# Two layers of a hybrid decoder: the weight sums' steps planned with a longer latency, and h's copy to DRAM written earlier in the FFN

## The chip, the core and the metric

The kernel runs on one core of a Trainium2 chip. A core has five engines that run side by side, each through its own queue of instructions in order: PE (TensorE, matmuls), DVE (VectorE), ACT (ScalarE), POOL (GpSimd) and SP (SyncE, which here only issues DMAs). They wait for each other by semaphores. POOL also issues DMAs; those that add to what stands in DRAM all come from it. The metric is the device time of one execution in microseconds (us), lower is better, as the median of several runs.

## The reference

The reference is two layers of a decoder on 16 + 512 = 528 positions of width 1024, all in float32. Each layer has a mixer and an FFN:

```python
u = rms_norm(h, pre_g); z = u @ w_in                    # mixer
q, k, v, f_logit, a_val, a_gate, sc_b, sc_c, sc_x = split(z)
y = concat[forgetting_attention(q, k, v, log_sigmoid(f_logit + b)),   # 8 heads of 64
           silu(layer_norm(conv31(a_val * sigmoid(a_gate)))) @ a_pw_w,
           sc_b * conv3(sc_c * sc_x)]
h = h + rms_norm(head_rms_norm(y) @ w_out, post_g)

z = conv3(rms_norm(h, ffn_pre_g) @ w_up)                # FFN, 2 x 2816 columns
g, up = split(z)
h = h + rms_norm((silu(g) * up) @ w_down, ffn_post_g)
```

The attention's logits are q.k/8 plus a running sum of log f, with a causal mask and a softmax. The output is h without the 16 first positions.

## The kernel before

**Matmuls.** Every float32 weight and every activation is split in two parts, hi and lo, and a product is three matmuls (hi*hi, hi*lo, lo*hi; `mm3`, L837). A weight block of 512 KB comes from DRAM by a DMA of SP into a tile raw, ACT casts it to whi, DVE subtracts to get wlo.

**Mixer.** `mixer` plans its work with `Flow`, a planner in Python that runs before the kernel: each operation has an engine, a planned duration, a priority, what it comes after, and `lat`, which is added to its planned end before what depends on it may be planned. The planner so fixes the order of the instructions on PE, DVE, ACT and POOL (`tc.manual_schedule`). The attention of a head has two passes. In `maxima` PE multiplies k by q (L1593), DVE takes the maximum of each row (mcol, L1600), POOL writes it on a diagonal (dm, L1608), and PE turns that into a row by a matmul with ones (L1617), which ACT puts into q as one more row (L1619). In `exponentials` PE multiplies again (L1637), ACT takes the exponential (pf, or p for the last 16 positions, L1644), POOL clears what lies above the causal diagonal (L1651), and PE multiplies by v (L1671). Between them PE runs the projections of q, k, v and the gates (L837, L1407). SP copies rows of q and k between partitions (L1499).

**FFN.** The 2816 columns are 22 pairs of blocks f (gate and up), in parts of 8, 7 and 7; behind each part come the down products of that part. 9 pairs in the first layer and 12 in the second (`SEVEN`) are computed by `seven_pair` with seven half products in place of eight (Strassen's scheme), which needs sums of weight blocks and of activations. The sums of activations are made by `normalised`, a generator of steps that `build` takes in small lots, five behind each of the first f, and the rest in the first down product; a step `None` ends a lot. From the end of part 0 on, h's tile serves as room for weight blocks, so h is copied to DRAM (h_dram, two DMAs of SP, L2385) and read back later (L2357).

**Weight sums.** A sum for pair f is a DRAM tile w_sum{layer}_{f}: SP copies three blocks into it (L545), then three accumulating DMAs of POOL follow (L534), each of which waits until the one before has landed. In the mixers these four steps are operations of the planner: 3 sums in the first mixer (11, 12, 13) and 4 in the second (10 to 13). In the plan, sum i is not begun before `SUM_EVERY * i` us, a step of POOL takes `SUM_US`, and the next one comes at least `SUM_LAT` behind it (L1846 to L1850). POOL's queue runs in order, so what stands behind an accumulate that waits for a landing waits too. The other sums are made in the FFNs (`tick`, `down_sums`) and are not planned by `Flow`.

Of the kernel before, what the change touches and what calls it, by code (L numbers as in the profile page):

```python
# [18 lines left out]
KD = D // P  # L19
# [13 lines left out]
        ((8, 9), (10, 11, 12, 13), (15, 16), (17, 18), (19, 20)))  # L33
SEVEN = tuple(sorted(sum(places, ())) for places in SUMS)
NEXT_SUMS, AHEAD_SPLITS = 13, (8, 8, 9, 9, 10, 10, 11)
SUM_US, SUM_LAT, SUM_EVERY = 0.9, 9.0, 40.0
K2 = KD // 2
SB = K2 * P
AHEAD = 2
# [350 lines left out]
def tile_hybrid_trunk(ctx: ExitStack, tc: tile.TileContext, xT, wflat, pv_d, out):  # L390
    nc = tc.nc
# [3 lines left out]
    def T(pool, shape, dt, tag, bufs=None):  # L395
        uid[0] += 1
        kw = {} if bufs is None else {"bufs": bufs}
        return pool.tile(list(shape), dt, tag=tag, name=f"{tag}_{uid[0]}", **kw)
# [83 lines left out]
    flow = Flow()  # L482
# [17 lines left out]
    h_dram = T(dram, [P, KD, L], F32, "h_dram")  # L500
# [25 lines left out]
    def sum_steps(l, f):  # L526

        gate, up = (flat_w(up_chunk[l, t]) for t in (f, NF + f))
        t = T(dram, [P, 4, SB], F32, f"w_sum{l}_{f}")
        n, o = P * 2 * SB, offs[up_chunk[l, f]]  # L530
        diag = wflat[o:o + 2 * (n + SB)].rearrange("(e q) -> e q", e=2)[:, :n].rearrange("e (p s) -> p e s", p=P)[:, :, :SB]

        def put(to, src):
            nc.gpsimd.dma_start(to, src, accum_op=ALU.add)  # L534

        def last():
            put(t[:, 3], t[:, 2])
            sums[l, f] = t

        moves = [(t[:, 0], up[:, :SB]), (t[:, 1], up[:, :SB]), (t[:, 2:4], gate.rearrange("p (e s) -> p e s", e=2))]  # L540

        def copies():
            with tc.issue_after(last_load[0].ins):
                for to, src in moves:
                    nc.sync.dma_start(to, src)  # L545

        return copies, lambda: put(t[:, 0:2], diag), lambda: put(t[:, 2], t[:, 1]), last

    def sums_at(l, place):

        return SUMS[l][place] if l < DEPTH else ()
# [143 lines left out]
    def gp(us, fn, *after, **kw):  # L695
        return flow.op("pool", us, fn, after, **kw)
# [428 lines left out]
    def mixer(l, ypool, first, close_first, spans, front, rzs, u_at):  # L1125
# [719 lines left out]

        for i, f in enumerate(sums_at(l, 1)):  # L1846
            copies, *adds = sum_steps(l, f)
            tok = flow.op("sp", 2.0, copies, (Tok(flow.pe + SUM_EVERY * i),), prio=8, lat=SUM_LAT)
            for op in adds:
                tok = gp(SUM_US, op, tok, prio=8, lat=SUM_LAT)  # L1850

# [177 lines left out]
    with tc.tile_pool(name="pre", bufs=2, reuse_waits="tile") as sp, tc.manual_schedule(engines=every):  # L2029
# [7 lines left out]
        h, h_at = load_h(sp, xT)  # L2037
# [56 lines left out]
    for l in range(DEPTH):  # L2094
# [23 lines left out]
        with tc.tile_pool(name=f"fp{l}", bufs=2, reuse_waits="tile") as fp:  # L2118
# [35 lines left out]
            with tc.manual_schedule(engines=every):  # L2154
                flow.yields = YF
                h, h_at = load_h(fp, xT if l == 0 else h_dram)
# [40 lines left out]
            seven = SEVEN[l]  # L2197
# [12 lines left out]
            def normalised():  # L2210

                pools.pop().close()
                st = ExitStack()
                pools.append(st)
                tp = tx[0] = st.enter_context(tc.tile_pool(name=f"tp{l}", bufs=1, side="right", reuse_waits="tile"))
                tiles = [T(tp, [P, 2, K2, n7], F32R, f"t{i}") for i in range(4)]
                gpre = gains("ffn_pre_g")
                skip = 2 * n7 - (L - i0)
                b11, b12, b21, b22 = blocks = [(k0, h7[hf]) for k0 in (0, K2) for hf in range(2)]

                def un(b, k):
                    k0, (a, z) = b
                    a += skip * (b in (b12, b22))
                    nc.vector.scalar_tensor_tensor(yp[:, k0 + k, a:z], in0=h[:, k0 + k, a:z], scalar=gpre[:, k0 + k:k0 + k + 1],
                                                   in1=rz[:, a:z], op0=ALU.mult, op1=ALU.mult)

                def at(b):
                    k0, (a, z) = b
                    return yp[:, k0:k0 + K2, a:z]

                def block(k):
                    c = (slice(None), slice(k, k + 2), slice(i0, L))
                    nc.scalar.copy(uhi[c], yp[c])
                    nc.vector.tensor_sub(ulo[c], yp[c], uhi[c].bitcast(F32))

                raw = {}

                def total(i, k, x, y, op=ALU.subtract):
                    raw[i] = T(fp, [P, 2, H], F32, "acc", 2)[:, :, :n7]
                    a, b = (t if t.shape[1] == 2 else t[:, k:k + 2] for t in (x(), y()))  # L2240
                    nc.vector.tensor_tensor(raw[i], in0=a, in1=b, op=op)

                def split(i, k):
                    hi, lo = (tiles[i][:, b, k:k + 2] for b in range(2))
                    nc.scalar.copy(hi, raw[i])
                    nc.vector.tensor_sub(lo, raw[i], hi.bitcast(F32))

                for b in (b12, b22, b11, b21):
                    for k in range(K2):
                        yield lambda b=b, k=k: un(b, k)  # L2250
                for k in range(0, K2, 2):
                    if k:
                        yield None
                        yield lambda: block(0)
                        yield None
                    yield lambda: total(2, k, lambda: at(b12), lambda: at(b22))
                    yield lambda: split(2, k)
                    yield lambda: total(0, k, lambda: at(b11), lambda: at(b12))
                    yield lambda: total(1, k, lambda: at(b22), lambda: raw[0], ALU.add)
                    yield lambda: split(0, k)  # L2260
                    yield lambda: total(3, k, lambda: at(b21), lambda: raw[1])
                    yield lambda: split(1, k)
                    yield lambda: split(3, k)
                for k in range(2, KD, 2):
                    yield lambda k=k: block(k)
                    yield None
                ts.extend((t[:, 0], t[:, 1]) for t in tiles)

            mul_ins, glo_ins, ghi_ins = [None], [None], {}
            ts, n_seven, primed = [], [0], set()  # L2270
            building = [None]

            def build(n):

# [64 lines left out]
            def finish_pair():  # L2339
                if late_ups:  # L2340
                    late_ups.popleft()()
# [3 lines left out]
            for part, nf in enumerate(PARTS):  # L2345
                for f in range(f0, f0 + nf):
                    if g:
                        tick(g[max(g)][0][:, :1])
                    for _ in range(AHEAD_SPLITS.count(f) if l == 0 else 0):
                        store_one()  # L2350
                    if f in seven:
                        seven_pair(f)
                        if f == seven[-1]:
                            spare[0] = None
                            with tc.issue_after(last_load[0].ins):
                                for k in range(0, KD, 2):
                                    nc.sync.dma_start(h[:, k:k + 2], h_dram[:, k:k + 2])  # L2357
                        continue
                    finish_pair()
                    if seven and f == 2:  # L2360
                        building[0] = normalised()
                    for i in (2 * f, 2 * f + 1):
                        if i < len(zs):
                            continue
                        if i < FIRST["w_out"]:
                            scaled(i, [first.ps[hf, i] for hf in range(2)])
                            continue
                        w = next_w()
                        ps = mmt((6, 2)[i % 2]) if ts else mmt()
                        mm3({hf: ps[:, hf, :iws[hf]] for hf in range(2)}, w, range(KD), u_in)  # L2370
                        if ts:
                            for (a, z), hf in zip(i_spans, range(2)):
                                nc.scalar.copy(zs[i % len(zs)][:, off + a - i0:off + z - i0], ps[:, hf, :z - a])
                            continue
                        scaled(i, [ps[:, :, :H]] if i0 == 0 else [ps[:, hf, :iws[hf]] for hf in range(2)])
                    g[f] = ffn_gate(f)
                    if building[0] is not None and f < PARTS[0] - 1:
                        with tc.issue_after(mul_ins[0].ins):
                            build(5)
                finish_pair()  # L2380
                ks = list(range(nf))
                grhs = lambda b, k, hf, f0=f0: g[f0 + k][b][:, fw * hf:fw * (hf + 1)]
                if seven and part == 0:
                    for k in range(0, KD, 4):
                        nc.sync.dma_start(h_dram[:, k:k + 4], h[:, k:k + 4])  # L2385
                    spare[0] = h
                if part < len(PARTS) - 1:
                    more = down_sums(l, part)
# [102 lines left out]
```

## Time and profile before

| | us |
|---|---|
| median of 3 runs | 1263.06 |
| lowest, highest | 1262.32, 1263.31 |
| profiled execution | 1262.1 |
| its span | 1260.4 |
| first mixer, about | 55 to 215 |
| first FFN with w_out and down products, about | 215 to 684 |
| second mixer, about | 684 to 842 |
| second FFN, about | 842 to 1260 |

The span runs from the first instruction to the last. In the prediction a row of a timeline is: start, duration, engine, line, operation, output <- inputs, sizes, and in brackets how long the engine was idle before it and what ended the wait. A row of waits is: engine, what it waited to start, for whom, then the total, how often, and the longest. A row of stretches is: the stretch, its length, then busy time and count for PE, PEld (weight loads), DVE, ACT and POOL, the granted clock of PE, the share of the DMA engines, and GB/s. A row of one line's instructions gives the least, median and longest duration in ns.

### The profile page before, as it was taken

What the parts mean: (1) busy time and instruction counts of PE and PEld (TensorE: products, weight loads), DVE (VectorE), ACT (ScalarE), POOL (GpSimd) and SP (SyncE); (2) the same over time, 40 slices, a digit from 0 to 9 for tenths busy, and PEclk for the clock granted to TensorE, in tenths of its full rate; (3) what the DMA queues carried; (4) which work ended last, traced back from release to release, by engine and by line L of the source; (5) the groups of instructions that cost most, each with busy time, mean ns of one, the idle gap of its engine ahead of it and who ended that gap; (6) DMA issues with size and microseconds to landing.
All of it is one profiled execution on the core that took longest, in us unless ns stands there. A gap on an engine that the chain in (4) does not pass through costs nothing.

```text
span 1260.4 us, 24292 instructions
## 1 busy us (share of the span) xinstructions
PE 1244.2 (99%) x9554; PEld 1194.4 (95%) x9554; DVE 926.0 (73%) x1581; ACT 710.3 (56%) x1377; POOL 175.9 (14%) x360
## 2 busy tenths in 40 slices
PE   8999999999999999999999999999999999999997
PEld 8999898999999999999999988999999899989997
DVE  7887866589874776487688877756799748757954
ACT  7254576655444663476673545775554447526763
POOL 1323411001111001010003244110022000000000
PEclk9999999999999999999999999999999999999999
DMA  7267551726658755765652684547166565465611
GB/s 245 80 154 180 122 118 47 256 88 150 185 146 339 243 192 153 243 193 169 209 186 68 157 194 109 144 116 238 70 166 177 148 212 172 151 228 178 203 60 67
DMA packets 80755, 206.59 MB, mean 164 GB/s; under 512 B 8624, under 2 KB 18992, under 8 KB 80128
## 3 DMA queue, kind: packets, MB, share of 16 engines
q1 hardware_dynamic: 66976, 168.20, 42.1%
q0 software_dynamic: 13664, 36.84, 13.0%
q8 instruction: 75, 1.23, 0.4%
q14 instruction: 40, 0.33, 0.1%
HBM read 170.82 MB, written 50.60 MB: 176 GB/s over the span
## 4 chain that ended last, share of the span: by engine, by line
PE 94%; DVE 2%; ACT 1%; DMA 1%; POOL 1%; issue 0%; SPq 0%; DVEq 0%; ACTq 0%
PE psum L837 63%; PE psum L2288 17%; PE psum L1407 5%; PE psum L1671 3%; PE psum L1637 2%; PE psum L974 1%; PE psum L1593 1%; PE psum L1737 1%; PE psum L1323 1%; DMA raw<-in_w_dram 0%; POOL dm L1608 0%; DMA h<-in_x_dram 0%; DVE yp L1050 0%; DVE h L1060 0%; PE psum L1617 0%
## 5 line engine op out<-in xcount | busy, mean ns | idle before, releaser
L837 PE MATMUL psum<-y,whi 128*128 128x264 f32 (+3 forms) x1968 | 383.8, 299 | 0.8 <-DVE zs L989 0.7
L837 PEld LDWEIGHTS psum<-y,whi 128*128 128x128 f32 x1968 | 305.8, 188 | 13.7 <-DVE zs L989 0.9
L837 PE MATMUL psum<-uhi,whi 128*128 128x264 f32 (+1 forms) x1168 | 292.2, 289 | 1.5 <-ACT uhi L2069 0.8
L837 PE MATMUL psum<-ulo,whi 128*128 128x264 f32 (+1 forms) x1168 | 286.0, 284 | 0.6 <-DVE ulo L2071 0.4
L837 PE MATMUL psum<-uhi,wlo 128*128 128x264 f32 (+1 forms) x1168 | 285.3, 284 | 0.0
L837 PE MATMUL psum<-y,wlo 128*128 128x264 f32 (+3 forms) x984 | 274.0, 297 | 0.7 <-DVE wlo L793 0.7
L837 PEld LDWEIGHTS psum<-uhi,whi 128*128 128x128 f32 x1168 | 201.7, 189 | 5.9 <-issue 1.6
L837 PEld LDWEIGHTS psum<-ulo,whi 128*128 128x128 f32 x1168 | 201.8, 189 | 1.3 <-DVE ulo L2071 0.6
L837 PEld LDWEIGHTS psum<-uhi,wlo 128*128 128x128 f32 x1168 | 201.5, 189 | 0.0
L837 PEld LDWEIGHTS psum<-y,wlo 128*128 128x128 f32 x984 | 178.0, 188 | 6.4 <-DVE wlo L793 1.1
L2173 DVE SCALAR_TENSOR_TENSOR c<-zs,pv,c 128x528 f32<-128x528 f32 (+1 forms) x176 | 130.5, 756 | 21.2 <-ACT c L2171 19.9
L652 ACT CAST whi<-raw 128x1024 fp32r<-128x1024 f32 (+1 forms) x65 | 66.1, 1021 | 96.9 <-PE psum L837 74.3
L793 DVE TENSOR_TENSOR wlo<-raw,whi 128x1024 fp32r<-128x1024 f32 (+2 forms) x80 | 95.6, 1204 | 31.1 <-ACT whi L789 30.5
L789 ACT CAST whi<-raw 128x1024 fp32r<-128x1024 f32 (+2 forms) x80 | 81.7, 1030 | 26.3 <-PE psum L837 18.1
L653 DVE TENSOR_TENSOR wlo<-raw,whi 128x1024 fp32r<-128x1024 f32 (+1 forms) x65 | 76.9, 1183 | 20.9 <-ACT whi L652 20.9
L1153 DVE SCALAR_TENSOR_TENSOR cacc<-apad,pv,cacc 128x528 f32<-128x528 f32 x120 | 87.5, 771 | 0.1
L2288 PE MATMUL psum<-uhi,whi 128*128 128x258 f32 (+1 forms) x252 | 71.4, 284 | 0.0
L2288 PE MATMUL psum<-ulo,whi 128*128 128x258 f32 (+1 forms) x252 | 71.3, 283 | 0.0
L2288 PE MATMUL psum<-uhi,wlo 128*128 128x258 f32 (+1 forms) x252 | 70.8, 283 | 0.0
L2171 ACT ACTIVATE c<-zs,pv 128x528 f32<-128x528 f32 (+1 forms) x88 | 63.0, 727 | 6.8 <-DVE zs L2136 2.6
L2206 POOL COPY cols<-y 128x1 f32<-128x1 f32 x24 | 18.4, 767 | 334.7 <-ACT y L2187 334.4
L2288 PE MATMUL psum<-t,shi 128*128 128x258 f32 (+1 forms) x336 | 63.2, 283 | 0.0
(273 smaller groups left out, 2324.4 us busy)
## 6 DMA issues: line engine op xcount, KB each, us to landing
raw<-in_w_dram SPq DMA_DIRECT2D x114, 512.0 KB, 4.6
raw<-in_w_dram SPq DMA_DIRECT2D x30, 448.0 KB, 5.2
h<-in_w_dram SPq DMA_DIRECT2D x25, 512.0 KB, 4.7
raw<-w_sum SPq DMA_DIRECT2D x21, 512.0 KB, 5.2
h<-w_sum SPq DMA_DIRECT2D x21, 512.0 KB, 5.1
h<-in_w_dram POOLq DMA_DIRECT2D x16, 512.0 KB, 4.0
w_sum<-h POOLq DMA_DIRECT2D x16, 512.0 KB, 6.3
w_sum<-in_w_dram SPq DMA_DIRECT2D x26, 256.0 KB, 5.8
```

The lines of the kernel that those rows point to most:

```text
L652: nc.scalar.copy(hi[:, :sz], raw[:, :sz])
L653: last_low[0] = nc.vector.tensor_sub(lo[:, :sz], raw[:, :sz], hi[:, :sz].bitcast(F32))
L789: nc.scalar.copy(box["hi"][:, :sz], box["raw"][:, :sz])
L793: nc.vector.tensor_sub(lo[:, :sz], box["raw"][:, :sz], box["hi"][:, :sz].bitcast(F32))
L837: nc.tensor.matmul(d, lhsT=w[a][:, k, cols], rhs=rhs(b, k, hf), start=start and i == 0 and p == 0, stop=stop and i == n - 1 and p == 2)
L1153: nc.vector.scalar_tensor_tensor(conv[j], in0=src, in1=conv[j], scalar=col("a_dw_w", CK * j + i), op0=ALU.mult, op1=ALU.add)
L1407: nc.tensor.matmul(ps[:n, :nw], lhsT=(uhi, ulo)[ui][:, k, P * b:P * b + n], rhs=w[wi][:, k % 4, :], start=k == 0 and p == 0, stop=k == KD ...
L1637: nc.tensor.matmul(s, lhsT=k[:, ka:ka + kn], rhs=q[:, s0:qz], start=i == 0, stop=i == 1)
L1671: nc.tensor.matmul(acc[:, s0 - qa:qz - qa], lhsT=vals[:, b].rearrange("p h d -> p (h d)")[:, o:o + P], rhs=box["p"], start=b == 0, stop=b ...
L2171: nc.scalar.activation(dst, src[:, 2:2 + 2 * fw], AF.Copy, scale=wtap(2, t))
L2173: nc.vector.scalar_tensor_tensor(dst, in0=src[:, i:i + 2 * fw], scalar=wtap(i, t), in1=dst, op0=ALU.mult, op1=ALU.add)
L2288: nc.tensor.matmul(psum[:, bank, :n7], lhsT=w[a][:, k0 + k, :], rhs=rhs(b, k), start=start and k == 0 and p == 0, stop=stop and k == K2 - ...
```

## The change

```diff
-SUM_US, SUM_LAT, SUM_EVERY = 0.9, 9.0, 40.0
+SUM_US, SUM_LAT, SUM_EVERY, SUM_SPAN = 0.9, 16.0, 40.0, 216.0
...
         for i, f in enumerate(sums_at(l, 1)):
             copies, *adds = sum_steps(l, f)
-            tok = flow.op("sp", 2.0, copies, (Tok(flow.pe + SUM_EVERY * i),), prio=8, lat=SUM_LAT)
+            tok = flow.op("sp", 2.0, copies, (Tok(flow.pe + min(SUM_EVERY, SUM_SPAN / len(sums_at(l, 1))) * i),), prio=8, lat=SUM_LAT)
             for op in adds:
                 tok = gp(SUM_US, op, tok, prio=8, lat=SUM_LAT)
...
                 for k in range(0, K2, 2):
                     if k:
-                        yield None
+                        if not downs:
+                            yield None
                         yield lambda: block(0)
                         yield None
...
-            building = [None]
+            building, downs = [None], []
...
                     if seven and f == 2:
                         building[0] = normalised()
+                    if seven and f in (2, 3):
+                        k = 4 * (f - 2)
+                        nc.sync.dma_start(h_dram[:, k:k + 4], h[:, k:k + 4])
...
                 finish_pair()
+                downs.append(part)
                 ks = list(range(nf))
                 grhs = lambda b, k, hf, f0=f0: g[f0 + k][b][:, fw * hf:fw * (hf + 1)]
                 if seven and part == 0:
-                    for k in range(0, KD, 4):
-                        nc.sync.dma_start(h_dram[:, k:k + 4], h[:, k:k + 4])
                     spare[0] = h
```

`SUM_LAT` rises from 9 to 16 us, so the planner sets the steps of a sum further apart; the beginning of sum i is limited by a new constant; `build` may leave out one pause once a part has reached its down products; and h's copy is written at f = 2 and f = 3. The FFN's instructions outside the planner are put in order by the scheduler of the framework, not by the text alone.

On POOL, in the first mixer, before the change. dm_98 and dm_99 are the two tiles dm, w_sum_12 a weight sum, pf the exponentials of one block of keys; of the last three pf rows the first clears a tile of 400 columns, the next one of 272, the last one of 144:

```order
L1608 TENSOR_SCALAR dm_98_728<-ident_75,mcol_1466 128x128 x3
L534 DMA w_sum_12_104_736<-w_sum_12_104_736 128x512
L1608 TENSOR_SCALAR dm_98_728<-ident_75,mcol_1466 128x128
L1651 AFFINE_SELECT pf_1568<-pf_1568 128x128
L1608 TENSOR_SCALAR dm_99_730<-ident_75,mcol_1566 16x16
L1608 TENSOR_SCALAR dm_99_730<-ident_75,mcol_1566 128x128 x4
L1651 AFFINE_SELECT pf_1652<-pf_1652 128x128
L534 DMA w_sum_12_104_736<-w_sum_12_104_736 128x512
L1651 AFFINE_SELECT pf_1665<-pf_1665 128x128
L1651 AFFINE_SELECT pf_1677<-pf_1677 128x128
```

The same stretch of POOL's queue in the changed kernel:

```order
L1608 TENSOR_SCALAR dm_98_728<-ident_75,mcol_1466 128x128 x4
L1651 AFFINE_SELECT pf_1567<-pf_1567 128x128
L1608 TENSOR_SCALAR dm_99_730<-ident_75,mcol_1565 16x16
L1608 TENSOR_SCALAR dm_99_730<-ident_75,mcol_1565 128x128 x4
L1651 AFFINE_SELECT pf_1651<-pf_1651 128x128
L1651 AFFINE_SELECT pf_1663<-pf_1663 128x128
L534 DMA w_sum_12_104_736<-w_sum_12_104_736 128x512
L1651 AFFINE_SELECT pf_1676<-pf_1676 128x128
```

The second step of w_sum_12 has gone from ahead of the last dm to between the last two pf, and the third has left the stretch (it stands where w_sum_13 began). The second mixer has the same rows with w_sum_11. The other moves on POOL, in each mixer, are: the second step of the first sum goes behind the first head's dm, where its third step stood; the first step of the sum behind w_sum_12 (w_sum_11) goes between two later pf; the last steps come later.

On PE, at the matmuls that take those pf, before the change:

```order
L1671 MATMUL psum_67<-pf_1665,vals_681 128x272
L1637 MATMUL psum_67<-q_94_708,k_86_700 16x16
L1637 MATMUL psum_67<-q_95_709,k_87_701 16x16
L1617 MATMUL psum_67<-dm_99_730,ones_r_80 128x264
L1407 MATMUL psum_67<-whi_1427,uhi_108 128x256
L1407 MATMUL psum_67<-whi_1427,ulo_109 128x256
L1407 MATMUL psum_67<-wlo_1446,uhi_108 128x256
L1671 MATMUL psum_67<-pf_1677,vals_681 128x144
L1407 MATMUL psum_67<-whi_1517,uhi_108 128x256
L1407 MATMUL psum_67<-whi_1517,ulo_109 128x256
L1407 MATMUL psum_67<-wlo_1536,uhi_108 128x256
```

And in the changed kernel, from the second group of L1407 on:

```order
L1407 MATMUL psum_67<-whi_1516,uhi_108 128x256
L1407 MATMUL psum_67<-whi_1516,ulo_109 128x256
L1407 MATMUL psum_67<-wlo_1535,uhi_108 128x256
L1671 MATMUL psum_67<-pf_1676,vals_681 128x144
L1617 MATMUL psum_67<-dm_99_730,ones_r_80 128x264
```

The matmul of the pf of 144 columns has gone behind the next three of L1407. This happens once in each mixer, and it is all that changes on PE.

On SP, around h's copy in the first FFN, before the change:

```order
L545 DMA w_sum_15_387_3552<-in_w_dram 128x1024
L650 DMA raw_3637<-in_w_dram 128x1024
L650 DMA raw_3720<-in_w_dram 128x1024
L2385 DMA h_dram_112<-h_2841 128x2112 x2
L650 DMA raw_3775<-in_w_dram 128x1024
```

And in the changed kernel:

```order
L545 DMA w_sum_15_387_3552<-in_w_dram 128x1024
L650 DMA raw_3638<-in_w_dram 128x1024
L650 DMA raw_3722<-in_w_dram 128x1024
L2365 DMA h_dram_112<-h_2841 128x2112 x2
L650 DMA raw_3777<-in_w_dram 128x1024
```

Only the line and the buffer numbers differ; SP's whole queue, DVE's and ACT's hold the same rows in the same order in both kernels.

## Prediction

> **What bounds the kernel now.** I read the page first (busy shares and the chain), then the table by stretches, then what TensorE (PE) waited for, then the timelines of the two mixers.
>
> ```profile
> span 1260.4 us, 24292 instructions
> PE 1244.2 (99%) x9554; PEld 1194.4 (95%) x9554; DVE 926.0 (73%) x1581; ACT 710.3 (56%) x1377; POOL 175.9 (14%) x360
> PE 94%; DVE 2%; ACT 1%; DMA 1%; POOL 1%; issue 0%; SPq 0%; DVEq 0%; ACTq 0%
> ```
> ```profile
> 55.00:215.00 160.00, 158.75 (x1179) 145.06 (x1178) 120.45 (x286) 95.08 (x247) 46.78 (x105) 1.00 0.52 122
> 684.00:842.00 158.00, 156.12 (x1158) 142.51 (x1157) 120.20 (x285) 95.25 (x247) 50.37 (x104) 1.00 0.59 137
> ```
> ```profile
> PE psum L1617 <- POOL dm L1608: 1.4, 2, 1.0
> PE psum L1671 <- POOL pf L1651: 0.6, 2, 0.3
> ```
>
> PE is busy for 1244.2 of 1260.4 us and carries 94% of the chain. The two stretches are the two mixers, where the weight sums lie; the first number behind the length is PE's busy time, so PE is without work for 1.25 and 1.88 us there. The last two rows are all that PE waited for POOL in the whole run: 1.4 + 0.6 = 2.0 us in four waits. In the mixers POOL has PE's work in its queue beside the weight sums: dm (L1608) feeds the matmuls of L1617, pf (L1651) those of L1671. So a POOL step that is planned elsewhere can win at most about 2 us, and only by making a dm or a pf earlier.
>
> The profiled execution took 1262.1 us, 1.7 more than its span; the median of the three runs, 1263.06, is 0.96 above that. A measurement of this kernel can tell about 0.2%, which is 2.5 us.
>
> **What the edits do to the instructions.** Of four edits two decide nothing. The spacing of the sums becomes min(40, 216/n), with n = 3 sums in the first mixer and 4 in the second: 216/3 = 72 and 216/4 = 54, so it stays 40. The pause that build() may skip in the first down product is reached before: normalised() gives 16 + 8 = 24 steps ahead of it, five builds of five steps at f = 2 to 6 take them all and reach the pause while downs is still empty. VectorE's (DVE) and ScalarE's (ACT) orders are the same rows in both kernels.
>
> The third, h's copy, moves in the text from behind f = 7 to f = 2 and 3, but not in SP's queue: its two rows stand behind the same two weight loads as before, with the same wait on DVE.
>
> ```profile
> 266.52 6.02 SPq L2385 DMA_DIRECT2D h_dram<-h  x2
> ```
>
> The trace puts the copy at 266.5 us, just behind the start of the FFN, long before the first down product. It was already early; I cost it at 0, and there is nothing that it could uncover, since what is queued behind it is unchanged.
>
> That leaves the fourth: the latency of a sum's step goes from 9 to 16 us, and with it POOL's order in both mixers, and one pair of matmuls on PE in each.
>
> **What is removed.** POOL's blocked waits behind an earlier accumulate:
>
> ```profile
> POOL w_sum L534 <- DMA w_sum<-in_w_dram: 20.3, 4, 6.6
> ```
> ```profile
> 66.22 0.89 POOL L534 DMA_DIRECT2D w_sum<-w_sum  x1 [6.63 <-DMA w_sum<-in_w_dram]
> 81.32 0.73 POOL L1608 TENSOR_SCALAR dm<-ident,mcol 16x16 fp32r<-16x16 f32 x2 [14.21 <-DVE mcol L1600]
> 694.22 0.85 POOL L534 DMA_DIRECT2D w_sum<-w_sum  x1 [5.87 <-DMA w_sum<-in_w_dram]
> ```
>
> One wait in each mixer, 6.63 and 5.87 us, goes: that accumulate now stands behind the first head's dm. But in the first mixer the dm behind it then waited 14.21 us more for DVE's mcol, so 12.5 us of POOL waiting are worth 0 on PE. The freed time turns into a longer wait for mcol.
>
> **What is moved.** Nine issues on POOL in the first mixer, twelve in the second; most land in a slot where another accumulate stood, or where POOL waits for mcol or an exponential for longer than an issue lasts. That duration (ns, least, median, most) is steady:
>
> ```profile
> L534 POOL DMA_DIRECT2D w_sum<-w_sum x26: 796/844/890, 66.2 to 984.7; - x26
> L534 POOL DMA_DIRECT2D w_sum<-in_w_dram x13: 1176/1196/1244, 58.3 to 964.4; - x13
> ```
>
> The first step of w_sum_13 (w_sum_12 in the second mixer), 1.20 us, comes between these two pf:
>
> ```profile
> 150.88 0.56 POOL L1651 TENSOR_SCALAR_AFFINE_SELECT pf<-pf 128x128 f32<-128x128 f32 x1 [6.13 <-ACT pf L1644]
> 152.58 1.43 POOL L1651 TENSOR_SCALAR_AFFINE_SELECT pf<-pf 128x128 f32<-128x128 f32 x2 [1.14 <-ACT pf L1644]
> ```
>
> The idle time there is 1.14, so the later pf comes 0.06 later at most, 0.12 in both mixers; I take 0, since PE shows no wait of that size. At the end of the second mixer POOL gains a wait of up to one landing behind the last accumulate; queued behind it is the COPY of L2206, which is not due for 80 us:
>
> ```profile
> 922.57 2.33 POOL L2206 COPY cols<-y 128x1 f32<-128x1 f32 x1 [84.22 <-ACT y L2187]
> ```
>
> One place per mixer is tight. The accumulate of w_sum_12 (w_sum_11 in the second) that stood ahead of the last dm of its head now stands between the pf of 272 and the pf of 144 columns, and PE takes the latter's matmul three L1407 matmuls later than before:
>
> ```profile
> 113.00 0.87 POOL L534 DMA_DIRECT2D w_sum<-w_sum  x1
> 125.08 0.34 POOL L1651 TENSOR_SCALAR_AFFINE_SELECT pf<-pf 128x128 f32<-128x128 f32 x1 [0.26 <-ACT pf L1644]
> 126.52 0.48 DVE L1307 SCALAR_TENSOR_TENSOR yta<-yta,pg,rs_t 128x264 f32<-128x264 f32 x1
> 127.26 1.22 DVE L793 TENSOR_TENSOR wlo<-raw,whi 128x1024 fp32r<-128x1024 f32 x1
> 126.33 0.28 PE L1407 MATMUL psum<-whi,uhi 128*128 128x256 f32 x1
> 126.68 0.41 PE L1671 MATMUL psum<-pf,vals 128*128 128x144 f32 x2
> ```
> ```profile
> 751.79 0.33 POOL L1651 TENSOR_SCALAR_AFFINE_SELECT pf<-pf 128x128 f32<-128x128 f32 x1 [0.27 <-ACT pf L1644]
> 753.23 0.48 DVE L1307 SCALAR_TENSOR_TENSOR yta<-yta,pg,rs_t 128x264 f32<-128x264 f32 x1
> 753.38 0.41 PE L1671 MATMUL psum<-pf,vals 128*128 128x144 f32 x2
> ```
>
> The pf of 272 ends at 125.08 + 0.34 = 125.42. I allow 0.05 for the step to the next op; this very accumulate took 0.87 at 113.00, so it stands from 125.47 to 126.34. The pf of 144, ready by then, follows; with the 0.34 of the row at 125.08 it ends at 126.68. PE asks for it at 126.68 plus three L1407 matmuls, which took 126.68 - 126.33 = 0.35: 127.03. Margin 0.35 us. In the second mixer: 752.12, accumulate 752.17 to 753.04, pf done 753.38, wanted at 753.38 + 0.35 = 753.73; again 0.35. The matmuls swapped on PE are the same, so the swap costs 0. **The sum: 0 removed from PE, 0 added**; the profiled execution would again take about 1262.1, and the median of runs 1263.0.
>
> **Rivals.** *DVE holds the late pf (slower).* A POOL op that starts beside a DVE op with two tensors from SBUF is held:
>
> ```profile
> 114.08 1.26 DVE L793 TENSOR_TENSOR wlo<-raw,whi 128x1024 fp32r<-128x1024 f32 x1
> 114.10 1.41 POOL L1608 TENSOR_SCALAR dm<-ident,mcol 128x128 fp32r<-128x128 f32 x1 [0.23 <-DVE mcol L1600]
> 114.84 0.28 PE L1617 MATMUL psum<-dm,ones_r 128*128 128x264 f32 x1
> 115.56 0.39 PE L1617 MATMUL psum<-dm,ones_r 128*128 128x264 f32 x1 [0.43 <-POOL dm L1608]
> ```
> ```profile
> 740.19 1.22 DVE L793 TENSOR_TENSOR wlo<-raw,whi 128x1024 fp32r<-128x1024 f32 x1
> 741.33 0.68 DVE L793 TENSOR_TENSOR pw<-raw,pw 128x512 fp32r<-128x512 f32 x1
> 740.21 1.97 POOL L1608 TENSOR_SCALAR dm<-ident,mcol 128x128 fp32r<-128x128 f32 x1 [0.21 <-DVE mcol L1600]
> 740.94 0.31 PE L1617 MATMUL psum<-dm,ones_r 128*128 128x264 f32 x1
> 742.23 0.40 PE L1617 MATMUL psum<-dm,ones_r 128*128 128x264 f32 x1 [0.98 <-POOL dm L1608]
> ```
>
> A dm that takes 0.37 elsewhere took 1.41, until 0.17 behind L793's end at 115.34; in the second mixer it was held through two DVE ops. The new pf starts at 126.34, DVE's L1307 at 126.52 (753.04 against 753.23). If the pf comes over 0.18 us later than I worked out, it is second. Held for L1307 alone it ends at 127.00 + 0.17 = 127.17, 0.14 late on PE, 0.3 in both mixers (1263.3). Held until the L793 behind it ends (127.26 + 1.22 = 128.48), it is there at 128.65, 1.62 late, 3.2 in both: 1266.2. For it: the margin is small and both mixers have it. Against it: both mixers keep their times to 0.02 us, and the pf is first in both. I give it 0.10, of which 0.04 is the full price. The Trainium skill, "SBUF — State Buffer", section "SBUF: two separate sides", says that the port pair of DVE and GpSimd is an exclusive lock and that whichever "starts first gets the pair for the whole instruction"; against a GpSimd op that reads SBUF this holds for DVE ops with two SBUF inputs too. By that rule a pf that is 0.18 ahead pays nothing and one that is 0.02 behind pays all; the trace agrees, the dm of 114.10 started 0.02 behind L793 and took 1.41.
>
> *The dm wins its race (faster).* The accumulate at 113.00 no longer stands ahead of that dm. If it had held the dm back, the dm would now go before L793. PE would gain 115.56 - 114.84 less the 0.12 between two plain matmuls (126.33 to 126.68 for three), 0.60, and 742.23 - 740.94 - 0.12 = 1.17: 1.8 together, 1261.3. Against it: the accumulate ended at 113.00 + 0.87 = 113.87, the dm started 0.23 later, and its row names mcol as what it waited for last. 0.07, and still within 0.2%.
>
> *A moved accumulate delays a copy of k (slower).* The transfer that starts at 126.3 lies on the last copies of k, used, I take it, by the head whose first product starts at 130.69:
>
> ```profile
> 125.26 1.19 SPq L1499 DMA_DIRECT2D k<-pair_lo  x2
> DMA to landing us min/median/max: 2.3/3.5/5.6
> 130.69 0.34 PE L1593 MATMUL psum<-k,q 128*16 128x16 f32 x2
> ```
>
> With the longest landing they are there at 126.45 + 5.6 = 132.05, 1.36 late, 2.7 in both mixers: 1265.7. Against it: the median landing gives 129.95, in time; the accumulate that now comes at 142 lay on these copies before (at 124), so one replaces another. 0.03.
>
> *The change does not do what it says.* For the spacing, the pause and the copy this is my forecast; for POOL's order it is not, the rows are different. Its time is the same 1263.0.
>
> **How the numbers follow.** Forecast of no change 0.78, at 1262.3 to 1263.7 (the spread of the three runs, moved by 0.4 either way); late pf 0.10 (0.06 at 1263.3 to 1264.5, 0.04 at 1266.2); dm 0.07 at 1261.3; k 0.03 at 1265.7; what is left, 0.02, is spread to the faster side. The range 1261.3 to 1264.5 leaves out 0.09. Faster by over 0.2% 0.02, slower by over 0.2% 0.07, within it 0.91.
>
> **What would show it.** In the changed profile: no POOL wait for w_sum ahead of the first dm of a mixer, and a wait for mcol near 14 + 7 = 21 us in its place; PE's waits for POOL still near 2.0 us in the same four rows; the pf of 144 columns done before PE's L1671 in both mixers; h's copy at 266.5 us; PE idle in the two stretches within 0.3 us of 1.25 and 1.88. The prediction is wrong if a pf of 144 shows over 0.5 us at that place with PE waiting behind it, if PE waits for a DMA in a mixer, or if time goes in an FFN, where I see no row that moved.

## The result, and the profile after

| | before | after |
|---|---|---|
| median of runs, us | 1263.18 (4 runs) | 1270.44 (4 runs) |
| lowest, highest | 1262.32, 1264.74 | 1269.82, 1270.92 |
| profiled execution, us | 1262.1 | 1270.35 |
| its span, us | 1260.4 | 1268.7 |

The changed kernel is slower: the ratio is 1.0056, with a 95% interval of 1.0038 to 1.0073. In the profiled executions the span is 8.3 us longer. The page of the changed kernel, with its head, the row of busy engines and the shares of the chain:

```profile
span 1268.7 us, 24292 instructions
PE 1247.7 (98%) x9554; PEld 1197.6 (94%) x9554; DVE 926.0 (73%) x1581; ACT 710.0 (56%) x1377; POOL 172.2 (14%) x360
PE 89%; DVE 3%; issue 3%; DMA 2%; ACT 1%; POOL 1%; SPq 0%; DVEq 0%; POOLq 0%; ACTq 0%
```

PE runs the same 9554 matmuls, but is busy for 3.5 us longer (1247.7 against 1244.2) and without work for 4.8 us longer (1268.7 - 1247.7 = 21.0, against 16.2). Together these are the 8.3 us, and both need an explanation. The two mixers as stretches:

```profile
55.00:215.00 160.00, 156.24 (x1146) 143.01 (x1145) 117.70 (x280) 92.29 (x239) 45.88 (x101) 0.99 0.49 122
684.00:842.00 158.00, 154.04 (x1140) 141.99 (x1139) 121.05 (x283) 89.27 (x230) 50.62 (x107) 0.99 0.54 133
```

PE is without work for 3.76 and 3.96 us there, where it was 1.25 and 1.88, and in both its mean clock fell from 1.00 to 0.99. PE's waits:

```profile
PE psum L1593 <- DMA k<-pair_lo: 2.9, 1, 2.9
PE psum L1593 <- issue: 2.5, 1, 2.5
...
PE psum L1617 <- POOL dm L1608: 0.6, 2, 0.4
...
PE psum L1671 <- POOL pf L1651: 0.6, 2, 0.3
```

The first two rows are new: one wait in each mixer at L1593, the product of q with k ("issue" means that the profile names nothing that ended it; what did is shown below). The two POOL rows, on which the prediction looked, got no longer. PE's timeline at the first of these waits:

```profile
109.50 0.28 PE L837 MATMUL psum<-uhi,wlo 128*128 128x264 f32 x1
112.32 0.34 PE L1593 MATMUL psum<-k,q 128*16 128x16 f32 x2 [2.54 <-issue]
...
113.06 0.42 PE L837 MATMUL psum<-ulo,whi 128*128 128x264 f32 x1
113.28 0.42 PE L837 MATMUL psum<-uhi,wlo 128*128 128x264 f32 x1
...
116.45 0.28 PE L837 MATMUL psum<-ulo,whi 128*128 128x264 f32 x1
116.57 0.28 PE L837 MATMUL psum<-uhi,wlo 128*128 128x264 f32 x1
```

PE stops for 2.54 us. Some 0.7 us after it starts again a matmul of 264 columns takes 0.42 instead of 0.28 us, and the next one starts 0.22 us behind it instead of 0.12, until about 116.4. The stretches with the granted clock (the first number behind the POOL column) say why:

```profile
109.70:112.30 2.60, 0.08 (x1) 0.01 (x1) 0.25 (x1) 0.00 (x0) 0.00 (x0) 1.00 1.07 294
112.30:114.00 1.70, 1.68 (x11) 1.70 (x12) 0.49 (x4) 0.00 (x0) 0.64 (x2) 0.70 0.87 206
114.00:116.30 2.30, 2.30 (x12) 2.30 (x12) 1.03 (x4) 0.00 (x0) 0.38 (x2) 0.50 0.17 51
```

During the wait the DMA engines are fully busy (share 1.07); behind it PE's clock is at half. The first dm of that head starts at 112.92 against 110.29 before, 2.63 late; its last dm starts at 118.25 against 114.10, 4.15 late. So in the first mixer the wait costs 2.6 and the slow clock another 1.5. The second mixer costs 3.6: a copy of q ahead of its wait starts at 727.71 against 723.14, 4.57 late, and a dm behind it at 752.81 against 744.62, 8.19 late. Its wait is longer (2.92), but PE waits for a dm there 0.77 less than before (0.21 against 0.98). The remaining 0.5 us or so is a longer wait in the first FFN (for zs, 0.86 at L2289 against 0.35 at L2288, the same instruction); it is as long in two kernels below that lose nothing (0.87 without the 512 KB step, 0.85 with plain copies), so it is no cost of the moved steps. What the DMA engines were busy with shows on POOL, after and then before:

```profile
101.81 0.87 POOL L534 DMA_DIRECT2D w_sum<-w_sum  x1
...
103.78 0.74 POOL L534 DMA_DIRECT2D w_sum<-in_w_dram  x1
112.92 0.27 POOL L1608 TENSOR_SCALAR dm<-ident,mcol 16x16 fp32r<-16x16 f32 x1 [8.39 <-DVE mcol L1600]
```
```profile
84.65 0.83 POOL L534 DMA_DIRECT2D w_sum<-w_sum  x1
...
101.19 1.19 POOL L534 DMA_DIRECT2D w_sum<-in_w_dram  x1
...
110.29 0.27 POOL L1608 TENSOR_SCALAR dm<-ident,mcol 16x16 fp32r<-16x16 f32 x1 [6.59 <-DVE mcol L1600]
```

Before, only the first step of w_sum_12 (512 KB) was issued here, at 101.19; the last step of w_sum_11 (256 KB) had gone at 84.65. Now that one comes at 101.81, and the 512 KB step 2.6 us later than before. SP issues the copies of k at the same time as ever, here after the change:

```profile
106.60 2.44 SPq L1499 DMA_DIRECT2D k<-pair_hi  x4
```

The view of DMA issues between 97 and 118 us (KB each, median us from issue to landing), after and then before:

```profile
k<-pair_hi SPq DMA_DIRECT2D x4, 132.0 KB, 5.5
...
w_sum<-in_w_dram POOLq DMA_DIRECT2D x1, 512.0 KB, 8.0
...
w_sum<-w_sum POOLq DMA_DIRECT2D x1, 256.0 KB, 6.9
```
```profile
k<-pair_hi SPq DMA_DIRECT2D x4, 132.0 KB, 2.6
w_sum<-in_w_dram POOLq DMA_DIRECT2D x1, 512.0 KB, 7.8
```

The copies of k land 5.5 us after issue instead of 2.6. 106.60 + 5.5 = 112.1, and PE goes on at 112.32. Before, 106.66 + 2.6 = 109.3, and PE used k at 109.68, 0.4 us later. These sums are estimates: in the first mixer the trace has a landing for the third of the six copies alone, and they take the first, which PE needs, to land as fast. In the second mixer the recorded landing is that of the first copy: 737.11 + 5.9 = 743.0 and PE goes on at 743.20, against 732.53 + 3.0 = 735.5 and 735.78 before. PE starts some 0.2 us behind a landing that it waits for, so before the change k had 0.2 us to spare at most. The second mixer's POOL and PE timelines show the same order of events:

```profile
732.54 0.87 POOL L534 DMA_DIRECT2D w_sum<-w_sum  x1 [0.21 <-issue]
734.52 0.73 POOL L534 DMA_DIRECT2D w_sum<-in_w_dram  x1
```
```profile
743.20 0.34 PE L1593 MATMUL psum<-k,q 128*16 128x16 f32 x2 [2.92 <-DMA k<-pair_lo]
```

This gives the **collision theory**: two accumulating transfers, 768 KB, now stand on the DMA engines right ahead of the copies of k; k comes late, PE stops, and the clock falls. Its rivals: one of the other edits costs; the moved issues hold POOL; one of the two transfers does it alone; the matmuls are slow for another reason than the gap.

### The profile page after: what moved, and what is told of

Read it like the earlier page. It is cut to its first block, busy times and chain, and to the rows that moved or that the text cites. A ratio compares the mean times of both kernels' runs of the same rounds, so it can differ in the third digit from the quotient of the medians.

```text
span 1268.7 us, 24292 instructions
## 1 busy us (share of the span) xinstructions
PE 1247.7 (98%) x9554; PEld 1197.6 (94%) x9554; DVE 926.0 (73%) x1581; ACT 710.0 (56%) x1377; POOL 172.2 (14%) x360
## 3 DMA queue, kind: packets, MB, share of 16 engines
q0 software_dynamic: 13664, 36.84, 12.6%
## 4 chain that ended last, share of the span: by engine, by line
PE 89%; DVE 3%; issue 3%; DMA 2%; ACT 1%; POOL 1%; SPq 0%; DVEq 0%; POOLq 0%; ACTq 0%
PE psum L837 59%; PE psum L2289 17%; PE psum L1407 5%; PE psum L1671 3%; PE psum L1637 2%; PE psum L974 1%; PE psum L1593 1%; DMA raw<-in_w_dram 1%; PE psum L1737 1%; PE psum L1323 1%; DMA w_split<-slo 0%; DMA h<-in_w_dram 0%; DMA h<-in_x_dram 0%; DVE yp L1050 0%; POOL dm L1608 0%
## 5 line engine op out<-in xcount | busy, mean ns | idle before, releaser
L2289 PE MATMUL psum<-uhi,whi 128*128 128x258 f32 (+1 forms) x252 | 71.3, 284 | 0.0
L2289 PE MATMUL psum<-ulo,whi 128*128 128x258 f32 (+1 forms) x252 | 71.2, 283 | 0.0
L2289 PE MATMUL psum<-uhi,wlo 128*128 128x258 f32 (+1 forms) x252 | 70.7, 283 | 0.0
L2289 PE MATMUL psum<-t,shi 128*128 128x258 f32 (+1 forms) x336 | 63.2, 283 | 0.0
```

The lines of the kernel that those rows point to most:

```text
L2289: nc.tensor.matmul(psum[:, bank, :n7], lhsT=w[a][:, k0 + k, :], rhs=rhs(b, k), start=start and k == 0 and p == 0, stop=stop and k == K2 - ...
```

## The experiments

All medians are beside runs of the kernel before on the same chip; the ratio need not be exactly that of the two medians. "Landing" is that of the copies of k in the first and the second mixer (about 106 and 734 us).

| kernel | median us | ratio to before, 95% interval | landing, us |
|---|---|---|---|
| after, lat 9 | 1263.88 | 1.0008, 0.9998 to 1.0017 | 3.5, 3.4 |
| before, lat 16 | 1270.48 | 1.0049, 1.0030 to 1.0069 | 6.2, 5.8 |
| first sum early | 1264.58 | 1.0012, 1.0001 to 1.0023 | 3.4, 3.1 |
| without the 512 KB step | 1262.22 | 0.9993, 0.9984 to 1.0003 | 2.4, 2.2 |
| plain copies | 1262.72 | 0.9994, 0.9985 to 1.0004 | 2.6, 2.8 |
| after, lat 14 | 1266.25 | 1.0022, 1.0012 to 1.0032 | 6.0, 3.8 |
| after, lat 13 | 1264.20 | 1.0005, 0.9996 to 1.0015 | 2.8, 3.7 |
| after, 22 idle matmuls | 1268.22 | 1.0037, 1.0024 to 1.0050 | 5.4, 5.7 |
| after again | 1271.35 | 1.0060, 1.0047 to 1.0072 | 6.8, 6.1 |
| after, 18 idle matmuls | 1267.86 | 1.0036, 1.0023 to 1.0050 | 6.3, 5.8 |

### All but the latency, and the latency alone

```diff
 # the changed kernel:
-SUM_US, SUM_LAT, SUM_EVERY, SUM_SPAN = 0.9, 16.0, 40.0, 216.0
+SUM_US, SUM_LAT, SUM_EVERY, SUM_SPAN = 0.9, 9.0, 40.0, 216.0
```

> The changed kernel with SUM_LAT back at 9.0; the spacing of the sums, the pause and the place of h's copy stay changed. Collision theory (the accumulates that the longer lat moves next to the copies of k cost it all): 1263.2 us, within 1.5, and no PE wait at L1593 for k. Rival, the other edits (spacing, pause, h's copy) carry the loss or part of it: 1265 to 1270. Rival, both parts are needed: 1263 too, but then lat 16 alone in the kernel before is also 1263.

```diff
 # the kernel before:
-SUM_US, SUM_LAT, SUM_EVERY = 0.9, 9.0, 40.0
+SUM_US, SUM_LAT, SUM_EVERY = 0.9, 16.0, 40.0
```

> The kernel before with SUM_LAT = 16.0 and nothing else. Collision theory: 1270.4 us, within 1.5, with one PE wait of 2.5 us or more at L1593 in each mixer. Rival, the other edits: 1263.2, or in between if they carry a part.

Measured: 1263.88 and 1270.48. The latency alone brings the whole loss, and the spacing, the pause and h's copy bring nothing that can be told from 0. Their traces agree: with lat 9 the engines run the same instructions in the same order as in the kernel before, and the kernel before with lat 16 runs those of the changed kernel. One part of the expectation was missed: with lat 9 PE does wait at L1593, for 0.92 and 0.44 us (the profile names copies of k from g_dram and pair_hi). That fits how little k has to spare. The kernel before with lat 16 has the two waits of PE:

```profile
PE psum L1593 <- issue: 3.3, 1, 3.3
PE psum L1593 <- DMA k<-pair_lo: 2.9, 1, 2.9
```

### Which of the two transfers

```diff
+LATS = ((9.0, 9.0, 9.0, 9.0), (16.0, 16.0, 16.0, 16.0))
...
+            lat = LATS[min(i, 1)]
-            tok = flow.op("sp", ..., lat=SUM_LAT)
-            for op in adds:
-                tok = gp(SUM_US, op, tok, prio=8, lat=SUM_LAT)
+            tok = flow.op("sp", ..., lat=lat[0])
+            for op, late in zip(adds, lat[1:]): tok = gp(SUM_US, op, tok, prio=8, lat=late)
```

> The changed kernel with the three steps of each mixer's first sum planned by 9.0 again and the rest by 16.0: on POOL one instruction moves in each mixer, the third accumulate (256 KB), back to where it stood before; PE, DVE, ACT and SP keep their order row by row. Collision theory in its first form, the third accumulate and the 512 KB step together make k late: k still shares the DMA engines with the 512 KB step, lands 3.5 to 4.5 us after issue and not 5.5, and the time is 1264 to 1267. Second form, the 512 KB step alone, 2.6 us later than before, suffices: 1268 to 1270. Third form, the third accumulate alone does it: 1263. POOL theory, the moved issue holds POOL and with it dm or pf: 1263 as in the third form, with k's landing unchanged at 5.5 us.

```diff
-            for op in adds:
-                tok = gp(SUM_US, op, tok, prio=8, lat=SUM_LAT)
+            for j, op in enumerate(adds):
+                tok = gp(SUM_US, (lambda: None) if (i, j) == (1, 0) else op, tok, prio=8, lat=SUM_LAT)
```

> The changed kernel without the first accumulate (512 KB from the weights) of each mixer's second sum: that part of the sum is left out of the computation; PE, DVE, ACT, SP keep their order row by row. Collision theory, first or second form: k lands in about 2.6 us, 1263 us, within 1.5. Third form (the third accumulate of the first sum does it, landing 6.9 us after 101.8): 1268 to 1270. Other-edits theory: 1270, unchanged.

With the first sum's steps back in their old places the time is 1264.58; without the 512 KB step, a part of the sum that this kernel leaves out, it is 1262.22. In the first mixer the third step goes back from 101.81 to 84.90, and the second from 84.75 to 66.74, which is over 20 us ahead of the copies of k in both places. In the first kernel the 512 KB step is still late (103.23), as its POOL timeline shows, but with nothing ahead of it, and in its view of DMA issues k lands in 3.4 us:

```profile
103.23 0.75 POOL L534 DMA_DIRECT2D w_sum<-in_w_dram  x1
```
```profile
k<-pair_hi SPq DMA_DIRECT2D x4, 132.0 KB, 3.4
```

PE waits 0.6 us at L1593 there in all, and k lands as fast as with lat 9 on that chip (3.5 us). So neither transfer does it alone: the 512 KB step in its late place without the other costs 1.5 us (0.1 to 2.9 by the interval of the ratio), and the 256 KB one without it nothing that can be told from 0. This is the first form of the theory, nearer to its lower end. POOL is no cause: for that k's landing would have had to stay at 5.5 us. Even without the 512 KB step the ratio, 0.9993, cannot be told from 1, so no run shows anything to win from another place for it.

### Bytes, or the accumulate

```diff
         def put(to, src):
-            nc.gpsimd.dma_start(to, src, accum_op=ALU.add)
+            nc.gpsimd.dma_start(to, src)
```

> The changed kernel with every step of the weight sums from GpSimd as a plain copy of the same bytes in place of an accumulate: the additions of these sums are left out of the computation; all engines keep their order. If it is the bytes that stand ahead of k (768 KB written at 101.8 and 103.8): k still lands 5 to 6 us after issue, 1268 to 1271. If it is the accumulate (256 KB lands in a median 5.0 us, where a plain copy of that size should be far faster): k lands within 3.5 us and the time is 1263, within 1.5.

Measured: 1262.72, k in 2.6 us. This kernel leaves the additions out. All its engines keep the order of the changed kernel, so neither POOL's new order nor PE's exchanged pair of matmuls carries the loss. And the bytes in the way are not enough; it is the adding. The queue of POOL's DMAs between 97 and 118 us (packets, MB, share of 16 engines' time), in the changed kernel and then with plain copies:

```profile
q0 software_dynamic: 416, 0.79, 24.8%
```
```profile
q0 software_dynamic: 224, 0.79, 12.6%
```

The same 0.79 MB takes twice the time on the DMA engines when it is added: 12.2% of 21 us are 2.6 us on each engine, about what k is late by (5.5 - 2.6 = 2.9). The Trainium skill, "DMA: Bandwidth & Descriptors", section "Issuing engines are not separate DMA queues", says that transfers of SyncE and GpSimd run on the same 16 engines and interleave; k's landing here agrees. The Trainium skill, "DMA: Bandwidth & Descriptors", section "Rules for kernel authors", says that an accumulate "reads its destination and writes it later", which fits the doubled time and packets.

### A smaller dose

```diff
-SUM_US, SUM_LAT, SUM_EVERY, SUM_SPAN = 0.9, 16.0, 40.0, 216.0
+SUM_US, SUM_LAT, SUM_EVERY, SUM_SPAN = 0.9, 14.0, 40.0, 216.0
```

> The changed kernel with SUM_LAT = 14.0: PE has the order of the kernel before, row by row; on POOL the third accumulate and the 512 KB step stand one and two rows earlier than with 16, with one 16-column pf step between them, so they are issued some 1 to 1.5 us sooner. Collision theory: both still run into the copies of k, which land 4 to 5 us after issue; PE waits 1 to 2 us in each mixer, with a small or no fall of the clock: 1265 to 1268. Rival, PE's pair that changes places with 16 (it does not here) carries the loss: 1263.

```diff
-SUM_US, SUM_LAT, SUM_EVERY, SUM_SPAN = 0.9, 16.0, 40.0, 216.0
+SUM_US, SUM_LAT, SUM_EVERY, SUM_SPAN = 0.9, 13.0, 40.0, 216.0
```

> The changed kernel with SUM_LAT = 13.0: PE has the order of the kernel before; the third accumulate stands five pf or p steps earlier than with 14 (near 95 us), the 512 KB step one step after p as with 14. Collision theory: the third accumulate is done before the 512 KB step begins, k lands within 3.5 us, 1263 to 1264.5. Rival (any change of lat from 9 that moves these steps costs): 1267 or more, near e7's time.

Measured: 1266.25 and 1264.20. With 14 the two issues come 0.7 and 1.4 us sooner than with 16; with 13 the third accumulate comes at 94.18, 8.05 us ahead of the 512 KB step. POOL's and PE's timelines with 14, then POOL's with 13:

```profile
101.11 0.86 POOL L534 DMA_DIRECT2D w_sum<-w_sum  x1
...
102.40 0.85 POOL L534 DMA_DIRECT2D w_sum<-in_w_dram  x1
```
```profile
112.58 0.34 PE L1593 MATMUL psum<-k,q 128*16 128x16 f32 x2 [2.83 <-issue]
...
114.02 0.29 PE L837 MATMUL psum<-uhi,whi 128*128 128x264 f32 x1
114.14 0.29 PE L837 MATMUL psum<-ulo,whi 128*128 128x264 f32 x1
```
```profile
94.18 0.87 POOL L534 DMA_DIRECT2D w_sum<-w_sum  x1
...
102.23 1.20 POOL L534 DMA_DIRECT2D w_sum<-in_w_dram  x1 [0.28 <-issue]
```

PE has the order of the kernel before in both, so its exchanged pair of matmuls carries none of the loss with 14 either. The times came as expected, but not every part: in the first mixer the wait with 14 is 2.83 us, not 1 to 2, and yet the clock stays at 1.00 behind it (matmuls 0.12 apart). In the second the wait is 0.9 us. 2.83 + 0.9 = 3.7 us, beside the 3.1 that the span has grown by (1263.5 against 1260.4). The length of the gap alone does not decide whether the clock falls; the last section shows what does.

### The clock by itself

In front of L1593, for the head that waits, in both mixers:

```diff
                         s, slot = yield from bank("s1")
+                        for _ in range(22 if hd == 2 and b == 0 else 0): nc.tensor.matmul(s[:, :H], lhsT=ones_r, rhs=dms[1][:, :H], start=True, stop=True)
                         s = s[:n, :z - a]
```

> The changed kernel with 22 idle matmuls of 264 columns (2.4 us at 0.11 each, on a tile that is ready, into the slot of psum that L1593 then overwrites) on PE just ahead of the L1593 that waits for k, in both mixers; the other engines keep their order. The copies land as late as before. Clock theory (the loss is the wait and, behind it, 1.5 us of matmuls at half the clock, in each mixer): the clock stays at 1.00 after 112 us and the time is 1267.4, some 3 us less than the changed kernel's 1270.4. Rival, the matmuls are slow for another reason (the same transfers, or the order of PE): 1270.4, unchanged, and the clock still falls. The other end: if the wait is shorter on this chip than 2.4 us, the idle matmuls themselves cost: 1271 to 1272.

Then the changed kernel once more, beside the same edit with `range(18 ...)`, on one chip:

> The changed kernel itself, unaltered, for a comparison on one chip with the next kernel. Clock theory: 1270.4 on average, but executions may differ by the 1.5 to 2 us that one fall of the clock costs, since the gap of 2.83 us with SUM_LAT 14 left the clock at 1.00: 1267 with no fall, 1269 with one, 1271 with two. Rival, the matmuls are slow for another reason than the gap: every execution 1270 to 1271.

> As the kernel with 22 idle matmuls ahead of L1593, with 18 (2.2 us), so that they end before k lands and cannot cost anything themselves. Clock theory: 0.3 to 0.6 us of wait for k is left behind them, the granted clock is 1.00 after it, 1267 to 1267.5 and 2 to 3.5 us under the changed kernel on the same chip. Rival: no difference from it.

Measured: 1268.22 with 22; 1271.35 for the changed kernel and 1267.86 with 18 on one chip, 3.5 us apart. k lands nearly as late (6.3 and 5.8 us with 18, beside 6.8 and 6.1 in the changed kernel there). Stretches behind the wait, in the changed kernel on this chip and then with 18 idle matmuls:

```profile
114.00:116.30 2.30, 2.30 (x12) 2.30 (x12) 0.39 (x3) 0.00 (x0) 0.63 (x2) 0.50 0.05 18
```
```profile
114.00:116.30 2.30, 2.30 (x20) 2.30 (x19) 1.33 (x7) 0.15 (x1) 1.04 (x3) 1.00 0.25 71
```

In 2.30 us PE does 20 matmuls instead of 12. The 3.5 us match the amount by which PE's busy time had grown (1247.7 - 1244.2), so the loss splits in two: the waits, and the half clock behind them. All ten executions with idle matmuls have a mean granted clock of 0.999 or 1.000, all nine of the changed kernel 0.996 or 0.997. The kernel with 18 still waits for k for 1.0 and 0.7 us where 0.3 to 0.6 was expected, since k was later on this chip (6.3 against 5.5 us). Executions of the changed kernel went from 1268.41 to 1272.83, and the fastest has the same mean clock as the slowest (0.997), so one fall of the clock more or less does not explain that spread; what does stays open. The kernel before with lat 16 does vary so: two executions at 0.995 and 0.996 took 1272.3 us, two at 0.998 and 0.999 took 1267.3 and 1268.7.

## Why the prediction was wrong

The forecast was 1263.0; 1270.44 was measured.

- **The spacing, the pause and h's copy at 0: right.** All but the latency gives a ratio of 1.0008, with 1 inside its interval.
- **POOL's removed waits worth 0: right.** The wait of 21 us for mcol that the prediction put in their place is there, and so is the harmless wait for the last accumulate behind the second mixer:

```profile
81.27 0.77 POOL L1608 TENSOR_SCALAR dm<-ident,mcol 16x16 fp32r<-16x16 f32 x2 [21.73 <-DVE mcol L1600]
...
850.79 0.80 POOL L534 DMA_DIRECT2D w_sum<-w_sum  x1 [3.90 <-DMA w_sum<-w_sum]
```

- **The tight place of the pf of 144 columns: right.** POOL's and PE's timelines of the changed kernel:

```profile
129.73 0.86 POOL L534 DMA_DIRECT2D w_sum<-w_sum  x1
130.32 0.59 POOL L1651 TENSOR_SCALAR_AFFINE_SELECT pf<-pf 128x128 f32<-128x128 f32 x1
```
```profile
131.24 0.41 PE L1671 MATMUL psum<-pf,vals 128*128 128x144 f32 x2
```

  It is done at 130.91 and wanted at 131.24, a margin of 0.33 where 0.35 was worked out. That the two agree is partly luck: the pf starts 0.59 us behind the accumulate's start, not 0.87, and takes 0.59, not 0.34. PE's waits for pf stay at 0.6.
- **The dm that might win its race: not so**, the last dm of that head still takes 1.41 us in both mixers (at 118.25 and 748.96, against 1.41 and 1.97 before). PE's waits for dm fell from 1.4 to 0.6 in all.
- **"Nine issues on POOL ... most land in a slot where another accumulate stood, or where POOL waits": this step failed.** It cost a moved step by the 0.8 to 1.2 us of its issue on POOL. The issue did fall into idle time of POOL, as it said. But each issue sends 256 or 512 KB through the DMA engines for 5 to 8 us, and that was followed for one place only. For the last step of w_sum_11 (84.65 to 101.81) and the first of w_sum_12 (101.19 to 103.78) the question of who shares the engines was not asked.
- **"A moved accumulate delays a copy of k": the right mechanism, in the wrong place, with too small a price.** It was put on the copies at 125.26, for which PE does not wait in the changed kernel, and priced with the longest landing of before (5.6 us) at 1.36 us a mixer. It happened at 106.6, where k had 0.2 us to spare, and cost waits of 2.54 and 2.92 us and, behind each, 1.5 us or more of half clock that was in no term. The rows for it were in the trace of before: the copies at 106.66 that land in 2.6, and L1593 at 109.68. With the accumulates of that trace (256 KB landing in a median 5.0 us, 512 KB in 7.7) issued near 102 one behind the other, an estimate is that the engines are not free before about 102 + 12.7 = 114.7: a k up to 5 us late, not one in time. (That is too long, since the two overlap: they landed at 101.81 + 6.9 = 108.7 and 103.78 + 8.0 = 111.8.)
- Its own sign for being wrong, "if PE waits for a DMA in a mixer", is the one that came.

No kernel here beats the one before by an amount that can be measured; the two that come out lowest leave work out.

## What to carry to other kernels

A step that issues a DMA has two costs when it is moved: the issue on its engine, which is short and easily hidden, and the transfer, which lies on all DMA engines for several us; list what else is in flight in that time and what slack each of these copies has (0.2 us or less here). Look for the copy with the least slack ahead of the engine that bounds the kernel, not for the place where the order of that engine changed. Where PE is the bound, price a stall by its length and by the slower clock that may follow it: here 2.6 and 1.5 us.

## What the runs showed of the hardware

**An accumulating DMA takes about twice the time of a plain one on the DMA engines**: 24.8% against 12.6% of 21 us for the same 0.79 MB. Over the whole kernel the median landing of POOL's 256 KB steps is 5.0 us as an add and 3.9 as a copy, and that of the 512 KB steps 8.0 and 5.0.

**A gap of 2.54 us is enough for the clock to fall, and one of 2.83 us can leave it; its place in time decides.** The clock fell to half behind gaps of 2.54, 2.88, 2.92, 3.22, 3.34 and 3.93 us, and did not behind 2.83 us with lat 14. The slow stretch is 3.41 us long each time (112.98 to 116.39 in the changed kernel). In each trace all changes of the granted clock lie whole multiples of 3.413 us apart: in the changed kernel it first rises at 7.17, and the changes at 112.98, 116.39, 744.44 and 747.86 come 31, 32, 216 and 217 times 3.413 us later. Cut into stretches of that length, the kernel with lat 14 (first rise at 5.13) has a boundary at 110.95, within its gap. These are the stretches around the first wait, in the changed kernel and then with lat 14:

```profile
109.57:112.98 3.41, 0.87 (x8) 0.69 (x8) 0.58 (x4) 0.00 (x0) 0.07 (x1) 1.00 1.06 287
112.98:116.39 3.41, 3.41 (x17) 3.41 (x16) 1.32 (x6) 0.00 (x0) 1.04 (x4) 0.50 0.35 82
```
```profile
107.53:110.95 3.42, 2.23 (x19) 2.02 (x17) 2.40 (x4) 0.39 (x1) 0.00 (x0) 1.00 1.03 212
110.95:114.36 3.41, 1.78 (x15) 1.81 (x16) 0.63 (x5) 0.00 (x0) 0.65 (x2) 1.00 0.85 218
```

In the changed kernel PE is busy for 0.87 of 3.41 us, idle for 74%, and the clock falls. With lat 14 the longer gap is split, 35% and 48% idle, and the clock stays. Ahead of the six falls PE was idle for 58% to 100% of such a stretch, and no stretch of these kernels that was idle for 57% or less is followed by a fall. That the place of the boundaries differs from run to run (first rise between 4.4 and 7.5 us in the twelve traces) would explain why executions of lat 14 have mean clocks from 0.997 to 1.000. No run moved a gap on purpose. The Trainium skill, "TensorE: Matmul & The Clock Gate", Part 1, says that a monitor judges PE's activity in free-running windows of 4096 cycles, 3.4 us; the traces agree, by the multiples of 3.413 us. The Trainium skill's rule on the same page, section "Why this matters for your kernels", of no gaps over about 3 us is too wide for this case: 2.54 us sufficed.
